# A runtime branch moved to the middle of the expert loop, with a deeper weight ring, in a two-layer decoder trunk

## The chip, the core and the metric

The kernel runs on one core of one Trainium2 chip, and its time is the device time in microseconds (us). Three executions took 850.05, 853.14 and 852.98 us; their median is 852.98 us. Engines are named as in the profile: PE (TensorE), PEld (its weight loads), DVE (VectorE), ACT (ScalarE), POOL (GpSimd) and SP (SyncE, which here does nothing but issue DMA transfers).

## The reference

One sequence of 256 tokens, 1024 features, passes two layers, all in float32. Layer 0 mixes tokens with a state-space scan, layer 1 with attention. Each layer ends in a mixture of 32 experts, of which every token uses two:

```python
for e in range(N_EXPERTS):                       # 32
    y = (jax.nn.silu(t @ w1[e]) * (t @ w3[e])) @ w2[e]
    out = out + gates[:, e:e + 1] * y            # gates: zero but for two experts per token
```

w1 and w3 are 1024x256 and w2 is 256x1024 for each expert, so the expert weights of a layer are 96 MB. Scale, shift and gate of each sub-layer come from `silu(c) @ ada_w`, with c one vector for the whole sequence.

## The kernel before

**The weight ring.** All large weights are cut into blocks of 1 MB, `[128, 2048]` in SBUF. A block is fetched by `fetch` (L66) into the next buffer of a ring (`new_slot`, L60): 10 buffers throughout (`ring=10`), to which a few more are added by `grow` while a stage has room (4 and then 5 more in the mixture of layer 0, 3 and then 4 more in that of layer 1). SP issues all these transfers in one queue; a transfer waits until its buffer's last reader is done, and for the landing of an earlier one that used the same of eight completion semaphores.

**The stages.** Layer 0 begins with the state-space part (the loop over 8 blocks below L990, most of its work on DVE), then an output gate, then its mixture; layer 1 has attention, then its mixture. At the very start SP is given the 8 blocks `ada00s`, then as many `win` blocks as the ring has room for (`ring - KD`), then the two tables `braw` and `craw` of the scan (L791, L792, 1 MB each), then the rest.

**The mixture** (`moe`). Every expert has a capacity of 32 tokens. Experts are taken in fours: `experts` loops over q = 0 to 7. In stage q `first` (L509) multiplies the gathered rows `xg` with 8 blocks `wa`, `second` (L524) with 4 blocks `wb`, DVE scales the result into `y` (L527) and `scatter` (L531) adds it into four PSUM banks `acc` with the one-hot matrix `Sc`. Meanwhile `place` (L459, L461) builds the one-hots of the next stage, `gather` (L473) multiplies the rows out for it, and `spread` multiplies its one-hots by the gates (L489, DVE), turns them on PE (L490) and copies them to `Sc`.

**The branch.** If an expert has more than 32 tokens, `overflow` (L538) computes the rest in the body of a runtime `If`, which is not entered with these inputs. It stands in program order in the last stage, q = 7, ahead of `first`: every engine reads the count (L622), compares and jumps. The body has its own transfers (SP, into the buffers of the tag "y") and its own matmuls, rows and copies; on the path that is not taken each engine instead raises its semaphores by what the body would have counted, after it has waited for what it had issued before.

**Order.** The scheduler of the framework orders each engine's instructions ahead of time by program order and by a model of their times; work may move past other work and past the branch, and the tiles of one tag are given out from a fixed number of buffers.

The line that the start depends on, and the buffers that the branch's body takes:

```python
for k in range(ring - KD if ring > KD else 0):
    prefetch("win", k)
...
w = mb[0].tile([128, 2, 512], F32, tag="y", name="ow", bufs=2)   # in overflow
```

## Time and profile before

| | us |
|---|---|
| median of three executions | 852.98 |
| the profiled execution | 851.51 |
| its span, first to last instruction | 849.7 |
| PE busy | 716.1 (84%) |
| DVE busy | 407.7 (48%) |
| DMA: 299.33 MB moved in the span | mean 352 GB/s |

The profiled execution is 1.47 us under the median, and 1.81 us longer than its span. PE is busy in most stages, but its busy time is an average over stages with different limits: what ends the waits differs between the state-space part, attention and the two mixtures. The DMA rate by slices of 21 us is the quickest way to tell them apart.

### The profile page before, as it was taken

The numbers are of one execution on the slowest core, as the hardware profiler recorded it, in microseconds if no ns is written. First come the engines' busy times: TensorE is split into PE (matmuls) and PEld (weight loads), VectorE is DVE, ScalarE is ACT, GpSimd is POOL, SyncE is SP. The second block draws the span as 40 slices with busy tenths as digits, with TensorE's granted clock in tenths as the row PEclk, the third lists the DMA queues.
The fourth block names the chain that finished last, engine by engine and source line by source line (L and its number), as shares of the span: only waits on it lengthen the run. The fifth ranks groups of instructions, "written<-read, shape, count | busy, mean of one in ns | idle before, by whom it ended". The sixth has DMA issues, their size and how long they took to land. (4 is left out here: it accounts for less than half of the span.)

```text
span 849.7 us, 13421 instructions
## 1 busy us (share of the span) xinstructions
PE 716.1 (84%) x5382; PEld 399.2 (47%) x5382; DVE 407.7 (48%) x1070; ACT 217.9 (26%) x498; POOL 51.5 (6%) x52
## 2 busy tenths in 40 slices
PE   3899999888999967866489999799888999887765
PEld 0676765663445312311245667788654443331211
DVE  7789999754223212110256579976644222221102
ACT  4334241442101101000143455566422111100100
POOL 2000000000000000000001104800200000000000
PEclk9999999999999998987699999999979999998888
DMA  9999676759999999999868988433889999999995
GB/s 372 426 424 390 248 297 250 306 214 424 427 427 426 425 427 427 426 425 426 341 252 324 341 299 297 154 145 115 316 330 370 426 427 425 427 427 427 426 425 213
DMA packets 41831, 299.33 MB, mean 352 GB/s; under 512 B 4632, under 2 KB 4760, under 8 KB 5664
## 3 DMA queue, kind: packets, MB, share of 16 engines
q1 hardware_dynamic: 41328, 297.13, 85.9%
q10 hardware_dynamic: 432, 1.25, 0.4%
q8 instruction: 46, 0.75, 0.3%
q14 instruction: 25, 0.20, 0.1%
HBM read 297.31 MB, written 1.05 MB: 351 GB/s over the span
## 5 line engine op out<-in xcount | busy, mean ns | idle before, releaser
L509 PE MATMUL mm<-w,xg 128*32 128x512 f32 x1024 | 138.0, 625 | 34.5 <-DMA w<-wa 23.0
L524 PE MATMUL mm<-w,aT 128*32 128x512 f32 x512 | 74.9, 705 | 16.2 <-DVE aT L499 7.4
L509 PEld LDWEIGHTS mm<-w,xg 128*32 128x32 f32 x1024 | 30.2, 111 | 116.8 <-issue 64.4
L531 PE MATMUL acc<-y,Sc 128*128 128x512 f32 x128 | 65.4, 636 | 22.6 <-DVE y L527 22.6
L1196 PE MATMUL acc<-ws,hn 128*128 128x512 f32 x288 | 76.4, 408 | 1.0 <-ACT hn L1164 0.8
L1126 DVE TENSOR_TENSOR ws<-w,ws 128x512 fp32r<-128x512 f32 x80 | 60.6, 764 | 30.2 <-ACT ws L1125 29.5
L473 PEld LDWEIGHTS mm<-Pr,h 128*128 128x128 f32 x512 | 61.4, 196 | 22.6 <-issue 20.6
L481 ACT ACTIVATE xg<-mm,sh,g 128x128 f32<-128x128 f32 x64 | 29.3, 457 | 162.8 <-PE mm L473 140.7
L515 DVE TENSOR_TENSOR a<-a,mm 128x256 f32<-128x256 f32 x16 | 6.7, 421 | 132.2 <-ACT a L514 132.2
L473 PE MATMUL mm<-Pr,h 128*128 128x128 f32 x512 | 65.9, 284 | 3.0 <-DVE Pr L461 3.0
L527 DVE TENSOR_TENSOR y<-mm,gbc 128x512 f32<-128x512 f32 x32 | 22.1, 692 | 92.8 <-PE mm L524 70.5
L1125 ACT ACTIVATE ws<-w 128x512 fp32r<-128x512 f32 x80 | 49.8, 628 | 63.3 <-PE acc L1196 42.4
L1196 PEld LDWEIGHTS acc<-ws,hn 128*128 128x128 f32 x288 | 51.6, 188 | 22.2 <-issue 5.5
L479 DVE TENSOR_SCALAR xg<-mm,g,sh 128x128 f32<-128x128 f32 x64 | 26.1, 407 | 73.7 <-ACT xg L481 73.7
L514 ACT ACTIVATE a<-mm 128x256 f32<-128x256 f32 x16 | 6.1, 383 | 192.8 <-PE mm L509 192.8
L531 PEld LDWEIGHTS acc<-y,Sc 128*128 128x128 f32 x128 | 22.6, 196 | 65.9 <-DVE y L527 38.3
L524 PEld LDWEIGHTS mm<-w,aT 128*32 128x32 f32 x512 | 15.4, 121 | 62.9 <-issue 35.3
L805 PE MATMUL mm<-hnT,w 128*64 128x128 f32 x512 | 32.2, 284 | 2.7 <-ACT hnT L278 2.7
L1390 PE MATMUL acc<-hn,ws 128*128 128x256 f32 x192 | 28.6, 307 | 6.6 <-DVE ws L1126 6.6
L805 PEld LDWEIGHTS mm<-hnT,w 128*64 128x64 f32 x512 | 30.4, 139 | 4.4 <-ACT hnT L278 3.7
L1390 PEld LDWEIGHTS acc<-hn,ws 128*128 128x128 f32 x192 | 26.3, 209 | 7.8 <-DVE ws L1126 7.5
L981 PE MATMUL acc<-w,uT 128*128 128x512 f32 x64 | 29.0, 596 | 0.7 <-ACT uT L970 0.7
(338 smaller groups left out, 963.5 us busy)
## 6 DMA issues: line engine op xcount, KB each, us to landing
w<-wa SPq DMA_DIRECT2D x128, 1024.0 KB, 19.6
w<-wb SPq DMA_DIRECT2D x64, 1024.0 KB, 19.6
w<-ada SPq DMA_DIRECT2D x36, 1024.0 KB, 10.8
w<-ada00s SPq DMA_DIRECT2D x8, 1024.0 KB, 13.6
w<-kvada SPq DMA_DIRECT2D x8, 1024.0 KB, 4.8
w<-win SPq DMA_DIRECT2D x4, 1024.0 KB
w<-ada00g SPq DMA_DIRECT2D x4, 1024.0 KB
w<-woutv SPq DMA_DIRECT2D x4, 1024.0 KB, 6.3
```

The lines of the kernel that those rows point to most:

```text
L473: PE.matmul(px[:, 128 * c4:128 * c4 + 128], h[:, i, 128 * c:128 * c + 128], Pr[:, i].rearrange("p a b -> p (a b)"), start=i == 0, stop=i == 1)
L479: V.tensor_scalar(xg[:, c], src, g[:, c:c + 1], sh[:, c:c + 1], op0=OP.mult, op1=OP.add)
L481: S.activation(xg[:, c], src, AF.Identity, bias=sh[:, c:c + 1], scale=g[:, c:c + 1])
L509: PE.matmul(ph[32 * s:32 * s + 32, :], xg[:, k, 32 * s:32 * s + 32], w[:, 512 * s:512 * s + 512], start=k == 0, stop=k == KD - 1)
L524: PE.matmul(py[32 * s:32 * s + 32, :], aT[:, 128 * f + 32 * s:128 * f + 32 * s + 32], w[:, 512 * s:512 * s + 512], start=f == 0, stop=f == 1)
L531: PE.matmul(acc[i][n], scs[q][:, 128 * i:128 * i + 128], y[:, 512 * n:512 * n + 512], start=q == 0, stop=q == NQ - 1, skip_group_check=True)
L805: PE.matmul(ps[64 * v:64 * v + 64, 128 * hh:128 * hh + 128], w[:, k, c0:c0 + 64], hnT[:, k, v::2], start=k == 0 and hh == 0, stop=k == KD ...
L981: PE.matmul(val[t][n], uT[:, m, 128 * t:128 * t + 128], wval[m // 2][:, c0:c0 + 512], start=m == 0, stop=m == 7)
L1125: S.activation(o[:, 0], w, AF.Copy)
L1126: V.tensor_tensor(o[:, 1], w, o[:, 0].bitcast(F32), op=OP.subtract)
L1196: PE.matmul(pk[i], src[:, k, a, 128 * i:128 * i + 128], w[:, b], start=k + a + b == 0, stop=k == KD - 1 and b == 1)
L1390: PE.matmul(po[:, 256 * m2:256 * m2 + 256], w[:, bb, kk, 128 * m2:128 * m2 + 128], hq[:, k, a, :], start=k + a + bb + m2 == 0, stop=k == K ...
```

## The change

The branch moves from q = 7 to q = 4, the middle of the loop. Its body's transfers no longer go into the tag "y" but into buffers of the weight ring (24 for one turn of its loop, where the mixtures have 21 and 19 of them); its normalised rows take the tag "y" instead of "xg", written by DVE; and it adds into `acc` instead of into `h`. "xg" has 2 buffers (was 3) and "P" 1 (was 2); `spread(q)` now stands ahead of `place(q + 1)`. The scratch for dynamic transfers is set to 1024 bytes, the vector `sc` is no longer copied 32 wide but read as a broadcast by PE, and the ring has 12 buffers instead of 10.

```diff
-def trunk(..., ring=10, ring2=4, ring3=5, ring4=3, ring5=4, lpb=2, TK=2):
+def trunk(..., ring=12, ring2=4, ring3=5, ring4=3, ring5=4, lpb=2, TK=2):
...
-    sc32 = const.tile([128, KD, 32], F32, name="sc32")
-    V.tensor_copy(sc32, sc[:, :, None].to_broadcast([128, KD, 32]))
+    def sc32(k):
+        return sc[:, k:k + 1].to_broadcast([128, 32])
...
-                PE.matmul(ps[32 * q:32 * q + 32, :], sc32[:, k, :], w[:, q], start=k == 0, stop=k == KD - 1)
+                PE.matmul(ps[32 * q:32 * q + 32, :], sc32(k), w[:, q], start=k == 0, stop=k == KD - 1)
...
-            return ma.tile([128, KD, 128], F32, tag="xg", name=n, bufs=3)
+            return ma.tile([128, KD, 128], F32, tag="xg", name=n, bufs=2)
...
-            P = mb[0].tile([128, 2, 4, CAP], F32, tag="P", name="P", bufs=2)
+            P = mb[0].tile([128, 2, 4, CAP], F32, tag="P", name="P", bufs=1)
...
-                hnT = [rows_tile("hnT") for _ in range(2)]
+                hnT = [mb[0].tile([128, KD, 128], F32, tag="y", name="hnT", bufs=2) for _ in range(2)]
                 for i in range(2):
-                    x = mb[0].tile([128, D], F32, tag="y", name="xn", bufs=2)
-                    V.tensor_scalar(x, h[:, i], rstd[:, i:i + 1], None, op0=OP.mult)
+                    x = mb[0].tile([128, 256], F32, tag="aT", name="dr", bufs=2)[:, 0:128]
+                    V.tensor_scalar(x, ident, rstd[:, i:i + 1], None, op0=OP.mult)
...
-                            PE.transpose(o, x[:, 128 * k:128 * k + 128], ident)
+                            PE.matmul(o, h[:, i, 128 * k:128 * k + 128], x, start=True, stop=True)
...
                         def part(name, j):
-                            w = mb[0].tile([128, 2, 512], F32, tag="y", name="ow", bufs=2)
+                            w = new_slot()[:, 0:1024].rearrange("p (k n) -> p k n", k=2)
                             nc.sync.dma_start(w, A[name][l, bass.ds(q, 1), 2 * j:2 * j + 2, :, c]
...
-                                add_gated(py[i], gbc, i, n, mb[0], "y", 2)
+                                for c2 in range(2):
+                                    r = slice(256 * c2, 256 * c2 + 256)
+                                    t = mb[0].tile([128, 256], F32, tag="aT", name="ot", bufs=2)
+                                    V.tensor_tensor(t, py[i][:, r], gbc[:, 512 * n + 256 * c2:512 * n + 256 * c2 + 256],
+                                                    op=OP.mult)
+                                    PE.matmul(acc[i][n][:, r], ident, t, start=False, stop=False,
+                                              skip_group_check=True)
...
-                if last:
+                if q == NQ // 2:
                     scatter(q - 1, y, 1)
                     overflow(nc.values_load(mosti[0:1, 0:1], min_val=0, max_val=T))
                 elif q:
...
+                spread(q)
                 if not last:
                     place(q + 1)
                     gather(q + 1)
-                spread(q)
                 aT = turned(a)
...
-    nc = bacc.Bacc("TRN2", target_bir_lowering=False, num_devices=1)
+    nc = bacc.Bacc("TRN2", target_bir_lowering=False, num_devices=1, dynamic_dma_scratch_size=1024)
```

## Rows read from the trace of the kernel before

**Rows 1.** The page: span, and GB/s in 40 equal slices.
```profile
span 849.7 us, 13421 instructions
...
GB/s 372 426 424 390 248 297 250 306 214 424 427 427 426 425 427 427 426 425 426 341 252 324 341 299 297 154 145 115 316 330 370 426 427 425 427 427 427 426 425 213
```

**Rows 2.** Two stretches: PE, PEld, DVE, ACT, POOL busy; clock, DMA share, GB/s.
```profile
50.00:150.00 100.00, 98.06 (x1384) 68.16 (x1380) 95.80 (x207) 33.61 (x93) 0.00 (x0) 1.00 0.77 310
285.50:401.90 116.40, 85.83 (x518) 27.79 (x516) 16.87 (x43) 7.02 (x16) 0.22 (x2) 0.88 1.01 426
```

**Rows 3.** Timeline of SP: first issue's start, time to the last one's end, count.
```profile
265.89 17.48 SPq L66 DMA_DIRECT2D w<-wa  x8
...
375.12 7.49 SPq L66 DMA_DIRECT2D w<-wb  x4
...
702.90 17.52 SPq L66 DMA_DIRECT2D w<-wa  x8
```

**Rows 4.** The page's DMA issues: count, KB each, median us to landing.
```profile
w<-wa SPq DMA_DIRECT2D x128, 1024.0 KB, 19.6
...
w<-kvada SPq DMA_DIRECT2D x8, 1024.0 KB, 4.8
```

**Rows 5.** The branch, line L538: ns min/median/max, first and last start in us.
```profile
L538 SPq EVENT_SEMAPHORE  x16: 17/17/17, 411.6 to 839.0; - x16
...
L538 PEldq COMPARE_BRANCH  x2: 545/3168/5790, 374.8 to 811.2; - x2
...
L538 SPq COMPARE_BRANCH  x2: 50/52/53, 392.4 to 818.5; - x2
```

**Rows 6.** Timeline, end of layer 0's mixture: start, length, [idle before <-releaser].
```profile
396.14 3.17 PE L524 MATMUL mm<-w,aT 128*32 128x512 f32 x16 [0.52 <-DVE aT L499]
...
412.35 0.69 DVE L527 TENSOR_TENSOR y<-mm,gbc 128x512 f32<-128x512 f32 x1 [16.27 <-SPq L538]
...
420.71 1.98 PE L531 MATMUL acc<-y,Sc 128*128 128x512 f32 x4 [0.82 <-DVE y L527]
```

**Rows 7.** Timeline, end of layer 1's mixture.
```profile
833.30 3.04 PE L524 MATMUL mm<-w,aT 128*32 128x512 f32 x16 [0.52 <-DVE aT L499]
...
839.21 0.69 DVE L527 TENSOR_TENSOR y<-mm,gbc 128x512 f32<-128x512 f32 x1 [5.97 <-SPq L538]
...
841.87 1.06 PE L524 MATMUL mm<-w,aT 128*32 128x512 f32 x8
...
843.75 1.98 PE L531 MATMUL acc<-y,Sc 128*128 128x512 f32 x4 [0.81 <-DVE y L527]
```

**Rows 8.** Lines L489 and L490 in layer 0's mixture, 190 to 420 us.
```profile
L489 DVE TENSOR_TENSOR P<-P,gates x16: 281/284/291, 204.5 to 326.3; 128x128 f32<-128x128 f32 x16
...
L490 PE MATMUL mm<-ident,P x16: 272/273/476, 215.4 to 384.1; 128*128 128x128 f32 x16
```

**Rows 9.** Timeline, the second y of stage 3 in layer 0 and layer 1.
```profile
287.05 0.69 DVE L527 TENSOR_TENSOR y<-mm,gbc 128x512 f32<-128x512 f32 x1 [3.10 <-PE mm L524]
...
724.57 0.69 DVE L527 TENSOR_TENSOR y<-mm,gbc 128x512 f32<-128x512 f32 x1 [3.10 <-PE mm L524]
```

**Rows 10.** Timeline of PE just behind the branch, layer 0 and layer 1.
```profile
380.92 2.95 PE L509 MATMUL mm<-w,xg 128*32 128x512 f32 x10 [3.60 <-issue]
...
817.43 3.64 PE L509 MATMUL mm<-w,xg 128*32 128x512 f32 x16 [4.75 <-PEq L538]
```

**Rows 11.** Timeline of the start: the scan's first table, and the loop's first product.
```profile
14.15 0.43 SPq L791 DMA_DIRECT2D braw<-s5b  x1
...
34.11 0.42 DVE L840 TENSOR_TENSOR abt<-braw,are 128x256 f32<-128x256 f32 x1 [1.59 <-DMA braw<-s5b]
...
48.23 0.69 DVE L918 TENSOR_TENSOR m<-mm,cosT 128x512 f32<-128x512 f32 x1 [2.22 <-PE mm L913]
```

**Rows 12.** Weight loads of a broadcast column (L206) and of a plain tile (L473).
```profile
L206 PEld LDWEIGHTS mm<-ident,sc x16: 190/190/192, 422.1 to 424.1; 128*128 128x128 f32 x16
...
L473 PEld LDWEIGHTS mm<-Pr,h 128*128 128x128 f32 x512 | 61.4, 196 | 22.6 <-issue 20.6
```

## The prediction

> **What bounds the kernel now.** I began with the page's DMA rate by slices. It stands at 424 to 427 GB/s for the first 60 us, through most of layer 0's mixture (slices 10 to 19) and of layer 1's (slices 32 to 39), and at 100 to 350 between them [rows 1]. Then two stretches by engine: in 100 us of the state-space loop DVE is busy 95.8 us, so DVE sets its pace; in the second half of layer 0's mixture DMA runs at 426 GB/s while PE is busy 85.8 of 116.4 us, so there the weights set it [rows 2]. The timeline of SP says the same: a load lands 19.6 us after its issue, which is eight 1 MB transfers in line [rows 4]. Stage 4's first block of layer 0 was issued at 265.89 and so landed at 285.5; the last of stage 7 at 375.12 + 7.49 - 0.33 = 382.3, landing at 401.9 [rows 3]. These are 47 blocks in 116.4 us, 2.48 each. Up to stage 3 it is PE's turn: the second y of stage 3 ends its wait by PE's product, at 287.05, when stage 4's first block had already landed [rows 3, 9].

> The branch shows last. In layer 0 PE's product for y was ready at 396.14 + 3.17 = 399.3, but DVE began at 412.35, ended by SP's line L538 [rows 6]. SP had reached the branch at 392.4 and raised its semaphores at 411.6 [rows 5]: 19.2 us, the time its eight transfers in line take to land. The branch's body writes buffers of tag "y" by DMA, so the y behind the branch waits for what SP raises. In layer 1 the same wait ends at 839.21, where the product was ready at 836.3 [rows 7].

> **The change, part by part.**

> 1. *The y wait goes.* Behind the branch y's buffers are no longer written by DMA. Without the wait, layer 0's end would run: y at 399.4 to 400.1, scatter (1.98) to 402.1, the products of the two last blocks (1.1 each; the last has landed at 401.9) to 404.3, y and scatter to 407.0. It ended at 420.71 + 1.98 = 422.7 [rows 6]: 15.7 us saved. In layer 1 the last scatter would begin at 841.3 in place of 843.75: y at 836.4, two products and a scatter by 840.6, y to 841.3; the last block has landed by 839.0, where SP's last semaphore is raised [rows 5, 7]. About 2.5 saved. Together -18.2. Late next are the weights themselves.

> 2. *The loads of stage 4 wait at the branch.* This decides. The body takes 24 ring buffers, more than there are, so each ring buffer's next load stands behind a reader in the body, and that reader's count is raised when PE passes the branch. Can loads be moved ahead of it? The trace shows one case of each kind: the multiplication by the gates for stage 7, which needs no new buffer, ran at 326.3, long before the branch; PE's transpose of its result, which needs a new PSUM buffer of the tag that the body also takes, ran at 384.1, behind it [rows 8]. Yet its input had been ready for 47 us, and PE idles in that stretch [rows 2]. I take the ring to be handled like that: stage 4's loads are issued only when PE is through. PE is through after stage 3's second y and its scatter: 287.05 + 0.69 + 0.06 + 1.98 = 289.8 in layer 0, 727.3 in layer 1 [rows 7, 9]. A load into an idle queue lands after 4.8 us, the median of `kvada` [rows 4]. So stage 4's first block lands at 289.8 + 0.1 + 4.8 = 294.7 instead of 285.5, and at 732.2 instead of 702.90 + 19.6 = 722.5 [rows 3]. From there the line of 48 blocks is unbroken and PE has a quarter of its time free [rows 2], so the ends move by the same: +9.2 and +9.7, +18.9 together. The bounds: -5 a layer if loads run ahead (first rival), +14 if PE's jump is slow too (second).

> 3. *Two more ring buffers.* They let SP be two blocks, 2 x 2.46 = 4.9 us, further ahead. But before the branch the last of stage 3 has then landed even earlier and DMA stands idle until PE arrives; and stages 0 to 3 do not wait for weights. In attention, DMA is far under its rate [rows 1]. I put 0, with -4.9 per mixture as the lower bound.

> 4. *The start.* Four `win` blocks instead of two stand ahead of the scan's tables in SP's queue, so these land 4.9 us later. DVE was already waiting for the first, 1.59 us until 34.11, and then had 2.22 us of idle time ahead of its first product at 48.23 [rows 11]. That gap and some shorter ones absorb about 2.7; I put +2.2, between 0 and 4.9. The loop behind it keeps DVE 96% busy and makes up nothing [rows 2].

> 5. *PE's own jump.* The branch instruction took 0.545 us in one layer and 5.79 in the other [rows 5], and PE's first product behind it waited 4.75 us for PE's sequencer in layer 1; in layer 0 a gap of 3.60 without a releaser came a few products later [rows 10]. Here the jump is issued before the last scatter ends and with DMA idle. I put +0.5 per layer; 0 to 4.4 each. [...]

> 6. *The small edits, 0 together.* A weight load of a broadcast column takes 190 ns, one of a plain tile 196 [rows 12], so reading `sc` as a broadcast costs PE nothing; it hides beside the products either way. One "P" and two "xg" buffers make `place(q + 1)` follow `spread(q)` in its own stage: DVE has 116.4 - 16.9 us idle there [rows 2] to cover it, and without that cover it would cost the four DVE operations, about 1 us a stage. The scratch size touches nothing in time: SP and ACT issue all transfers of this kernel, POOL none.

> The sum: -18.2 + 18.9 + 2.2 + 1.0 = +3.9 against the profiled execution's 851.51 (its span of 849.7 and 1.81 around it): **855.4 us**. That execution is 1.5 under the median of 852.98, so the forecast is 0.3% over the median. About 0.5%, 4.3 us, is what a measurement of this kernel can tell from no change.

> **The rivals.**

> *Loads run ahead of the branch, as they do now* (faster). For it: SP's loads of stage 7 and later were issued before its own branch at 392.4 in this trace, from 375.12 on [rows 3, 5]. Against it: those took buffers that the body did not. Then only SP's wait for its own eight transfers remains, and the queue restarts in 4.8 instead of 2.46, +2.4 a layer; the two buffers give -4.9 a layer. 851.5 - 18.2 + 2 x (2.4 - 4.9) + 2.2 gives **831 us**. A part of it, with some loads let through, lies between.

> *PE's jump stalls in both layers* (slower). The mechanism sits at the new place of the branch: SP's loads wait for PE, so what PE's sequencer loses there is lost by DMA too, while at the old place it was covered, since the weights were late anyway. Price: 4.75 against 0.4 us, +4.35 a layer in place of 0.5: 855.4 + 7.7 = **863 us**. It decides from the point where the jump takes more than the 1.5 us by which it is issued ahead of the scatter's end (811.2 against 817.43 - 4.75 = 812.7 in layer 1) [rows 5, 10]. For it, layer 1's 5.79; against it, layer 0's 0.545 and the idle queue.

> *The start costs its whole 4.9 us* (slower): 855.4 + 2.7 = **858 us**. For it: DVE 96% busy; against it: the 2.22 gap.

> **How the numbers follow.** My forecast 0.45, loads running ahead 0.27, slow jumps 0.20, the whole start 0.08. The forecast's own range is 849 to 859, of which I put 0.36 within 0.5% of the median, 0.07 above and 0.02 below. Faster: 0.27 + 0.02 = 0.29. Slower: 0.07 + 0.20 + 0.08 = 0.35. Same: 0.36. The range runs from 836, inside the first rival's upper part (0.12 of its 0.27), to 864: 0.45 + 0.12 + 0.16 (of the second rival's 0.20) + 0.08 = 0.81.

> **What would show it.** Right: DVE's y after the branch waits for PE alone; DMA idle for some 12 to 15 us ahead of stage 4 in each mixture; SP's first load of stage 4 released by PE; the scan's first table landing near 39 us; layer 0's mixture ending near 419 in place of 422.7, layer 1's about 7 later against its own beginning. Wrong: an unbroken DMA rate across the middle of the mixtures (first rival), or a branch instruction of PE over 4 us in both layers (second). The forecast also fails if stages 0 to 3 become shorter, since the branch is then reached earlier.

## The result and the profile after

The changed kernel takes 879.35 us (median of 4 runs, 877.41 to 880.9) against 852.91 for the kernel before in the same comparison: a ratio of 1.0305 (95% interval 1.0273 to 1.0338). It is slower by 3%, where 855.4 had been forecast with a range of 836 to 864. Line numbers of the changed kernel are one higher around the mixture and seven higher in the state-space part: the branch is L539, the y L528, the scatter L532.

First the page of the changed kernel: its span, and the DMA rate in 40 slices of 21.9 us.

```profile
span 877.2 us, 13392 instructions
...
GB/s 374 424 428 306 320 190 260 308 250 356 426 427 426 92 362 427 426 426 427 427 426 426 308 302 261 192 152 108 344 335 423 426 426 91 373 429 426 427 427 266
```

Where [rows 1] had an unbroken 424 to 427 through both mixtures, slices 14 and 34 now stand at 92 and 91. At a full rate of 427 these two and their neighbours (362 and 373) miss 20.5 us of DMA in layer 0 and 20.0 in layer 1. That is the hold which step 2 of the prediction described, and it is longer than the 12 to 15 us expected.

How much of the time this explains shows once the span is cut at two events of each layer: the write of `mosti` by DVE, from which the routing is known, and the end of the last scatter by PE. The timeline of DVE, kernel before:

```profile
196.30 0.15 DVE L438 CAST mosti<-most 128x1 int32<-128x1 f32 x1
...
632.22 0.15 DVE L438 CAST mosti<-most 128x1 int32<-128x1 f32 x1
```

The timeline of DVE, changed kernel:

```profile
210.13 0.15 DVE L439 CAST mosti<-most 128x1 int32<-128x1 f32 x1
...
648.23 0.15 DVE L439 CAST mosti<-most 128x1 int32<-128x1 f32 x1
```

The timeline of PE, changed kernel; the last scatters of the kernel before end at 422.69 and 845.73 [rows 6, 7]:

```profile
433.13 1.98 PE L532 MATMUL acc<-y,Sc 128*128 128x512 f32 x4 [1.21 <-DVE y L528]
...
871.21 1.98 PE L532 MATMUL acc<-y,Sc 128*128 128x512 f32 x4 [0.81 <-DVE y L528]
```

The differences of these times, in us, with the forecast's terms beside them:

| part | before | after | change | forecast |
|---|---|---|---|---|
| start, to `mosti` of layer 0 | 196.3 | 210.1 | +13.8 | +2.2 |
| mixture of layer 0 | 226.4 | 225.0 | -1.4 | -6.0 |
| attention and routing of layer 1 | 209.5 | 213.1 | +3.6 | 0 |
| mixture of layer 1 | 213.5 | 225.0 | +11.5 | +7.7 |
| output | 4.0 | 4.0 | 0 | 0 |
| span | 849.7 | 877.2 | +27.5 | +3.9 |

The mixtures miss the forecast by 8.4 us together, attention by 3.6, and the start by 11.6. So the largest error arises in the start, most of it in the first 100 us, far ahead of the branch that the prediction was mostly about.

The branch's own rows, line L539 (ns min/median/max, first and last start in us):

```profile
L539 SPq EVENT_SEMAPHORE  x16: 17/17/17, 281.5 to 731.8; - x16
L539 SPq COMPARE_BRANCH  x2: 50/52/53, 272.1 to 712.8; - x2
...
L539 PEldq COMPARE_BRANCH  x2: 3502/3696/3890, 304.8 to 742.5; - x2
...
L539 PEldq EVENT_SEMAPHORE  x2: 51/51/51, 308.4 to 746.5; - x2
```

In layer 0 SP reaches the branch at 272.1 and raises its eight semaphores from 281.5 to 291.5, yet it issues nothing until PE is through. This is the timeline of SP around the branch of layer 0:

```profile
264.36 7.71 SPq L66 DMA_DIRECT2D w<-wb  x4
308.47 5.42 SPq L66 DMA_DIRECT2D w<-wa  x8
```

PE's semaphore goes up at 308.4, and the first load of stage 4 is issued at 308.47. The timeline of PE shows what follows, with the last scatter ahead of the branch and the first product behind it, in layer 0 and in layer 1:

```profile
303.91 1.98 PE L532 MATMUL acc<-y,Sc 128*128 128x512 f32 x4 [0.81 <-DVE y L528]
313.81 1.93 PE L510 MATMUL mm<-w,xg 128*32 128x512 f32 x8 [7.92 <-DMA w<-wa]
...
742.01 1.98 PE L532 MATMUL acc<-y,Sc 128*128 128x512 f32 x4 [0.81 <-DVE y L528]
751.70 1.94 PE L510 MATMUL mm<-w,xg 128*32 128x512 f32 x8 [7.70 <-DMA w<-wa]
```

PE stands for 7.9 and 7.7 us: its own jump of 3.5 and 3.9, and a load into an empty queue. The scatters end at 305.9 and 744.0 and PE's semaphore goes up at 308.4 and 746.5, so the jump adds 2.5 us to the hold in each layer. PE also comes to the branch later than before, as the second y of stage 3 in the timeline of DVE shows for both layers:

```profile
303.17 0.69 DVE L528 TENSOR_TENSOR y<-mm,gbc 128x512 f32<-128x512 f32 x1 [3.96 <-PE mm L525]
...
741.27 0.69 DVE L528 TENSOR_TENSOR y<-mm,gbc 128x512 f32<-128x512 f32 x1 [3.96 <-PE mm L525]
```

That is 93.0 us after the routing in both; before it was 90.7 and 92.4 [rows 9].

The y wait of 16.27 us [rows 6] is gone; at the end of layer 0 DVE waits for PE's product alone, as its timeline shows:

```profile
427.34 0.69 DVE L528 TENSOR_TENSOR y<-mm,gbc 128x512 f32<-128x512 f32 x1 [3.71 <-PE mm L525]
```

Now the start. The timeline of DVE has the first table, the scan loop's first product, and the sum of a gate's product with its bias (L192):

```profile
39.61 0.43 DVE L847 TENSOR_TENSOR abt<-braw,are 128x256 f32<-128x256 f32 x1 [7.35 <-DMA braw<-s5b]
...
53.56 0.69 DVE L925 TENSOR_TENSOR m<-mm,cosT 128x512 f32<-128x512 f32 x1 [0.86 <-PE mm L920]
...
74.68 0.68 DVE L192 TENSOR_TENSOR rows<-mm,rows 128x512 f32<-128x512 f32 x1
```

The table comes 5.5 us later than in [rows 11], the first product 5.3. The engine that connects the two is ACT. Its timeline in the kernel before, which the prediction didn't read:

```profile
40.48 2.62 ACTq L184 DMA_DIRECT2D rows<-gbias  x2
43.15 0.51 ACT L852 ACTIVATE ab<-braw 128x128 f32<-128x128 f32 x2 [11.20 <-DMA w<-ada00g]
```

and in the changed kernel:

```profile
45.40 2.62 ACTq L185 DMA_DIRECT2D rows<-gbias  x2
48.07 0.39 ACT L814 ACTIVATE uT<-mm 128x256 f32<-128x256 f32 x1 [16.39 <-DMA w<-ada00g]
```

ACT has two small transfers of `gbias` to issue. Its idle time around them, 11.20 and 16.39 us, is ended by the landing of a 1 MB block `ada00g`, and the second issue begins 2.4 us behind the first in both kernels (42.87 and 47.79), where a block takes 2.46 at 426 GB/s. ACT's copies for PE, and through PE all of the loop, stand behind that. Another 5 us go at 75 us, where PE waits for the sum of L192 (it ends at 75.36; the view names ACT). The timeline of PE has both stops:

```profile
48.70 1.11 PE L868 MATMUL mm<-ident,ab 128*128 128x128 f32 x4 [5.63 <-ACT ab L859]
...
75.47 3.55 PE L198 MATMUL mm<-rows,pick 128*128 128x512 f32 x4 [3.34 <-ACT rt L936]
```

A part of the start's loss goes with TensorE's granted clock. Here are three stretches of the changed kernel, then one of the kernel before (length; busy time of PE, PEld, DVE, ACT, POOL; granted clock, DMA share, GB/s):

```profile
48.00:54.80 6.80, 5.91 (x42) 5.21 (x43) 3.93 (x12) 2.99 (x9) 0.00 (x0) 0.50 1.01 428
75.30:78.70 3.40, 3.23 (x4) 1.18 (x4) 3.36 (x10) 1.86 (x3) 0.00 (x0) 0.50 0.13 53
164.00:167.40 3.40, 3.40 (x66) 2.97 (x56) 0.27 (x1) 0.18 (x1) 0.00 (x0) 0.50 0.56 169
...
33.60:187.00 153.40, 146.90 (x1844) 108.77 (x1841) 131.56 (x280) 55.88 (x142) 0.00 (x0) 1.00 0.77 310
```

The granted clock stands at 0.50 from the end of both stops, in which PE was idle for 5.6 and 3.3 us, and once more at 164 us; in the kernel before it is 1.00 from 33.6 to 187 us. The timeline of PE has the same 64 products at either level, changed kernel first:

```profile
163.74 3.42 PE L975 MATMUL mm<-m,cz 128*32 128x128 f32 x64
...
151.82 1.95 PE L968 MATMUL mm<-m,cz 128*32 128x128 f32 x64
```

These products alone account for 1.5 of the 13.8 us; what the other two stretches cost was not separated from the stops.

### The profile page after: what moved, and what is told of

Same layout as the page of the kernel before. It is cut to its first block, busy times and chain, and to the rows that moved or that the text cites. A ratio compares the mean times of both kernels' runs of the same rounds, so it can differ in the third digit from the quotient of the medians.

```text
span 877.2 us, 13392 instructions
## 1 busy us (share of the span) xinstructions
PE 735.0 (84%) x5382; PEld 400.0 (46%) x5382; DVE 410.5 (47%) x1069; ACT 218.6 (25%) x498; POOL 57.8 (7%) x52
## 5 line engine op out<-in xcount | busy, mean ns | idle before, releaser
L510 PE MATMUL mm<-w,xg 128*32 128x512 f32 x1024 | 146.0, 651 | 49.3 <-DMA w<-wa 49.2
L510 PEld LDWEIGHTS mm<-w,xg 128*32 128x32 f32 x1024 | 27.8, 112 | 139.5 <-DMA w<-wa 69.8
L474 PE MATMUL mm<-Pr,h 128*128 128x128 f32 x512 | 65.4, 282 | 11.4 <-DVE Pr L462 11.4
L532 PE MATMUL acc<-y,Sc 128*128 128x512 f32 x128 | 63.8, 622 | 8.5 <-DVE y L528 8.5
L1203 PEld LDWEIGHTS acc<-ws,hn 128*128 128x128 f32 x288 | 51.1, 188 | 23.9 <-issue 7.1
L528 DVE TENSOR_TENSOR y<-mm,gbc 128x512 f32<-128x512 f32 x32 | 22.1, 692 | 73.2 <-PE mm L525 72.9
L493 DVE COPY Sc<-mm 128x256 f32<-128x256 f32 x16 | 6.8, 425 | 93.3 <-PE mm L491 93.3
L532 PEld LDWEIGHTS acc<-y,Sc 128*128 128x128 f32 x128 | 22.2, 193 | 51.6 <-issue 29.0
L1130 POOL TENSOR_TENSOR w<-w,gbc 128x512 f32<-128x512 f32 x16 | 32.5, 2066 | 0.0
## 6 DMA issues: line engine op xcount, KB each, us to landing
w<-ada00s SPq DMA_DIRECT2D x8, 1024.0 KB, 16.4
```

The costliest lines, as they stand in the source:

```text
L474: PE.matmul(px[:, 128 * c4:128 * c4 + 128], h[:, i, 128 * c:128 * c + 128], Pr[:, i].rearrange("p a b -> p (a b)"), start=i == 0, stop=i == 1)
L510: PE.matmul(ph[32 * s:32 * s + 32, :], xg[:, k, 32 * s:32 * s + 32], w[:, 512 * s:512 * s + 512], start=k == 0, stop=k == KD - 1)
L532: PE.matmul(acc[i][n], scs[q][:, 128 * i:128 * i + 128], y[:, 512 * n:512 * n + 512], start=q == 0, stop=q == NQ - 1, skip_group_check=True)
L1130: G.tensor_tensor(w, w, gate, op=OP.mult)
L1203: PE.matmul(pk[i], src[:, k, a, 128 * i:128 * i + 128], w[:, b], start=k + a + b == 0, stop=k == KD - 1 and b == 1)
```

## The experiments

All ratios are to the kernel before, run beside. The parts of each span are cut as above, from the profiled execution:

| kernel | time | ratio, 95% interval | start | mixture 0 | attention | mixture 1 |
|---|---|---|---|---|---|---|
| before | 852.9 | | 196.3 | 226.4 | 209.5 | 213.5 |
| after | 879.35 | 1.0273 to 1.0338 | 210.1 | 225.0 | 213.1 | 225.0 |
| e1_two_win | 873.88 | 1.0191 to 1.0271 | 208.7 | 224.0 | 212.4 | 223.7 |
| e2_no_branch | 831.38 | 0.9704 to 0.9764 | 209.2 | 207.1 | 206.4 | 204.1 |
| e3_own_tag | 840.58 | 0.9808 to 0.9885 | 208.5 | 207.8 | 208.4 | 210.0 |
| e4_before_no_branch | 832.26 | 0.9687 to 0.9792 | 198.4 | 209.4 | 207.7 | 210.9 |
| e5_ring10 | 856.03 | 1.0022 to 1.0067 | 196.8 | 222.1 | 209.0 | 222.9 |
| e6_own_tag_gbias_early | 828.94 | 0.9700 to 0.9755 | 197.8 | 210.7 | 206.2 | 209.6 |
| e7_own_tag_ring10 | 838.00 | 0.9818 to 0.9892 | 196.6 | 212.1 | 206.1 | 212.6 |
| e8_last_stage | 854.36 | 0.9991 to 1.0050 | 210.3 | 218.0 | 209.2 | 213.2 |
| e9_no_branch_ring10 | 829.87 | 0.9682 to 0.9785 | 196.6 | 211.0 | 205.9 | 209.3 |
| e10_pool_queue | 822.38 | 0.9604 to 0.9677 | 196.7 | 204.4 | 209.0 | 204.7 |
| e11_gbias_early | 864.97 | 1.0095 to 1.0171 | 196.3 | 227.2 | 213.4 | 224.2 |
| e12_before_pool_queue | 837.91 | 0.9763 to 0.9872 | 196.5 | 210.9 | 212.2 | 211.3 |

### The start: e1, e5 and e11

**e1_two_win.** Four `win` blocks ahead of the tables become two again, and the ring stays at 12.

```diff
-    for k in range(ring - KD if ring > KD else 0):
+    for k in range(2):
         prefetch("win", k)
```

> The changed kernel with one edit: only two blocks of `win` are fetched ahead of the scan's tables, as the kernel before did, with the ring still at 12. Theory S (the start is lost to the order of SP's loads: two more 1 MB blocks stand ahead of the tables, 4.9 us, and the state-space part gives up more behind that): the routing is known near 197.3 us as before instead of 211.1, and the time falls by 12 to 14 us, to 865 to 867. Rival T (the start is lost to the other edits of that part, above all the multiplications that read `sc` as a broadcast column): within 3 us of 879.35.

It gave 5.5 us, and the routing was known at 208.7: neither theory. The first table is loaded as early as in the kernel before, and yet ACT stands as long as in the changed one. Its timeline in e1_two_win:

```profile
45.45 2.60 ACTq L185 DMA_DIRECT2D rows<-gbias  x2
48.10 0.51 ACT L859 ACTIVATE ab<-braw 128x128 f32<-128x128 f32 x2 [16.29 <-DMA w<-ada00g]
```

So the late table isn't the cause; theory S had the wrong place.

**e5_ring10.** The changed kernel with `ring=10`, nothing else.

> The changed kernel with 10 ring buffers in place of 12, all else as changed, the branch in the middle too. Theory S2 (what the start loses comes from the longer ring: SP runs two loads further ahead of ACT, and ACT, which issues two small transfers of `gbias`, is held until later loads have landed, 45.4 instead of 40.5): the first product of the scan is back near 48.3 us, the routing is known at 197 to 199, and the time falls by 12 to 14 us to 865 to 868. Rival T (the broadcast column in the multiplications): the routing stays at 209 to 211, and the time within 3 us of 879.35. Both: the holes in the middle of the mixtures stay, shorter by up to 4.9 us on their early side, with no gain from that.

It took 856.03 us, 23.3 less than with 12 buffers and more than the 12 to 14 of theory S2; the start went back to 196.8, so rival T falls, and the broadcast column costs nothing that can be seen. ACT's timeline here is that of the kernel before to 0.1 us:

```profile
40.57 2.60 ACTq L185 DMA_DIRECT2D rows<-gbias  x2
43.22 0.51 ACT L859 ACTIVATE ab<-braw 128x128 f32<-128x128 f32 x2 [11.02 <-DMA w<-ada00g]
```

and DVE's timeline has the first product at its old time and the sum of L192 13.6 us earlier than in the changed kernel, ahead of a scan instead of behind it:

```profile
48.30 0.69 DVE L925 TENSOR_TENSOR m<-mm,cosT 128x512 f32<-128x512 f32 x1 [2.22 <-PE mm L920]
...
61.06 0.68 DVE L192 TENSOR_TENSOR rows<-mm,rows 128x512 f32<-128x512 f32 x1
```

Counted in the timelines of SP and ACT, 23 transfers are issued ahead of the first `gbias` in the kernel before and in e5_ring10, 25 in the changed kernel and in e1_two_win. In all four the transfer eight places ahead of that `gbias` is an `ada00g` block, which is what ACT stands for: the first of them in the kernel before, in e5_ring10 and, two places later in line, in the changed kernel, the third in e1_two_win. With 12 buffers two more loads fit ahead of `gbias`, whichever they are, and ACT stands two loads, 4.9 us, longer. This fits four kernels; that an issue waits for the eighth transfer before it was not tried by itself.

**e11_gbias_early.** The changed kernel with the two `gbias` transfers issued at the very start into a tile of their own; the gate's function takes that tile.

```diff
+    rows00 = sp.tile([128, 512], F32, name="rows00")
+    G.memset(rows00, 0.0)
+    for n in range(2):
+        nc.scalar.dma_start(rows00[32 * n:32 * n + 1, :], A["gbias"][0, n:n + 1, :])
     for k in range(KD):
         prefetch("ada00s", k)
...
-    side = [ada_gate_pe("ada00g", 0, 0, gb00, True),
+    side = [ada_gate_pe("ada00g", 0, 0, gb00, True, rows00),
```

> The changed kernel with one edit: the two small transfers of `gbias` are issued at the very start into a tile of their own. Body of the branch on the ring, 12 ring buffers, branch in the middle. Theory L (with the longer ring the start is lost to ACT, which stands at that issue, and to nothing else): the routing known near 198 us in place of 210.1, the time 879.35 less 11 to 13: 866 to 869, mixtures and attention as in the changed kernel (225, 213, 225). Rival V (the 9 us that the longer ring costs behind the start, by e5_ring10, also come from the shifted order of the start): 855 to 861.

The routing was known at 196.3 and the time fell by 14.4 us to 864.97, with four `win` blocks still ahead of the tables. That is theory L, a little more than it asked. Mixtures and attention stay as long as in the changed kernel, against rival V. The second stop at 75 us went too; it came of the same shift of order. PE's four products behind the sum of L192 took 1.99 us here and 1.98 in e5_ring10, as in the kernel before (1.98), where the changed kernel took 3.55 at a granted clock of 0.50. What stays open is why the longer ring costs another 9 us behind the start, 864.97 against 856.03: in the profiled executions 5.1 in layer 0's mixture, 4.4 in attention, 1.3 in layer 1's. Of the 5.1 and the 1.3, 2.0 and 1.2 have been lost by the second y of stage 3, before the branch.

### The hold at the branch: e2, e9, e3 and e8

**e2_no_branch.** The call of `overflow` is left out.

```diff
-                    overflow(nc.values_load(mosti[0:1, 0:1], min_val=0, max_val=T))
```

> The changed kernel without the branch: the part for overfull experts is left out altogether, and nothing stands in the middle of the mixtures. Theory H (SP's loads are held at the branch until PE has passed it, and PE's jump adds to that): no hole in the DMA rate within a mixture. Layer 0's mixture takes the 225.4 us of before less the y wait of 15.7, less 0 to 4.9 for the two ring buffers, layer 1's 216.8 less 2.5 less the same, against 225 and 228 in the changed kernel: 30 to 39 us less, 840 to 849. Rival O (the mixtures are longer because of the order `spread` then `place` and the fewer buffers): a gain of less than 11 us, above 868.

831.38 us, 48.0 less than the changed kernel; the mixtures shrank by 17.9 and 20.9, attention by 6.7. That is theory H, though the gain is some 9 us more than its 840 to 849 asked.

**e9_no_branch_ring10.** The same with `ring=10`.

> The changed kernel without the branch and with 10 ring buffers: the part for overfull experts is left out altogether. Theory H (the branch in the middle, with 10 buffers too, costs the hold of the loads and PE's jump, and the other edits cost nothing): mixtures of about 209 and 211 us as in e4_before_no_branch, 222.1 and 222.9 in e5_ring10, so 856.0 less 25, plus or minus 3: 828 to 834. Rival O (the order `spread` then `place`, one `P` and two `xg` buffers make the mixtures longer): 836 or more.

829.87, inside theory H's 828 to 834. Against e4_before_no_branch, 832.26, the small edits (order of `spread` and `place`, fewer `P` and `xg`, broadcast column) cost nothing that can be told where no branch stands. Against e2_no_branch the start is 12.6 shorter and the mixtures are 3.9 and 5.2 longer: without the branch the longer ring gives back most of what it takes from the start (831.38 against 829.87).

**e3_own_tag.** The branch's body loads into a buffer of its own.

```diff
-                            w = new_slot()[:, 0:1024].rearrange("p (k n) -> p k n", k=2)
+                            w = mb[0].tile([128, 2, 512], F32, tag="ow", name="ow", bufs=1)
```

> The changed kernel with one edit: the body of the branch loads its weights into one buffer of a tag of its own (4 KB) and takes no ring buffer. The branch stays in the middle. Theory H1 (the loads are held because they use ring buffers that the body also takes): SP then waits at the branch only for its own transfers in line, the hole in the DMA rate shrinks from 20 to 22 us to about 5 in both layers, and the time falls by about 2 x 16 us, to 843 to 853. Rival H2 (SP is held until PE is through the branch whatever the body writes): within 3 us of 879.35. A value between would say that PE's jump, 3.5 and 3.9 us, is what is left.

840.58, 38.8 less with the branch still in the middle: theory H1, and 2.4 us below its range. The page's DMA rate:

```profile
GB/s 371 426 425 304 345 165 252 282 344 282 426 427 426 426 424 426 350 425 429 426 426 427 424 302 270 152 188 125 293 313 410 427 426 428 419 367 378 425 428 272
```

The holes of 92 and 91 are gone; 350 in slice 17 and 367 and 378 in slices 36 and 37 are left, some 4 to 6 us of DMA per layer, where SP waits for its own transfers in line. PE's jump has become longer in the same kernel (line L539):

```profile
L539 PEldq COMPARE_BRANCH  x2: 5942/6760/7579, 303.2 to 719.1; - x2
```

It costs nothing in layer 0, where the mixture is as short as without a branch (207.8 and 207.1), since the weights are what is waited for; in layer 1 the mixture stays 5.9 longer than without a branch (210.0 and 204.1), and how much of that is the jump was not separated. So the hold comes from the shared buffers, and not from the place of the branch alone.

**e8_last_stage.** The changed kernel with the branch put back.

```diff
-                if q == NQ // 2:
+                if last:
```

> The changed kernel with the branch put back to the last stage, all else as changed (its body on the ring, 12 ring buffers). Theory D (a hold at the branch costs the distance by which the loads run ahead of PE there: 15 to 20 us in the middle, where PE sets the pace of stages 0 to 3, and little at the last stage, where PE waits for each load): 831.4, the time without a branch, plus 5 to 9 us per layer, so 841 to 850. Rival W (at the last stage the loads are held by SP's own eight transfers in line, 16 to 19 us, as the y was): 862 to 870. If the place makes no difference: within 3 us of 879.35.

854.36, between the two: 25.0 less than in the middle, but dearer than theory D. The rows of L539 show the same hold at the new place:

```profile
L539 SPq EVENT_SEMAPHORE  x16: 17/17/17, 380.0 to 807.5; - x16
L539 SPq COMPARE_BRANCH  x2: 50/52/53, 360.9 to 787.9; - x2
...
L539 PEldq COMPARE_BRANCH  x2: 3315/3356/3396, 383.4 to 810.7; - x2
```

In layer 0 SP's last semaphore goes up at 380.5, PE's at 386.9. The mixtures are 10.9 and 9.1 us longer than in e2_no_branch, in the middle 17.9 and 20.9. Counted from the routing, the first load behind the branch is issued 34.3 and 34.1 us later than in e2_no_branch when the branch stands in the middle, and 23.9 and 24.1 later when it stands in the last stage: the loads run further ahead of PE in the middle, and the hold costs more there.

### The old wait: e4 and e12

**e4_before_no_branch.** The kernel before without its call of `overflow`.

> The kernel before without the branch: the part for overfull experts is left out. It prices the y wait that the prediction put at 15.7 and 2.5 us. Theory Y (the wait is on the path in full): 852.9 less 18.2 is 834.7, so 832 to 838. Rival Z (the weights of attention land during the wait, so that part of it is given back later): 840 to 853, with the attention part longer than its 210.2 us of before by what is given back.

832.26: theory Y. The mixtures shrank by 17.0 and 2.6 us, where the prediction had put the y wait at 15.7 and 2.5.

**e12_before_pool_queue.** The kernel before with the transfers in the branch's body on another queue.

```diff
-                            nc.sync.dma_start(w, A[name][l, bass.ds(q, 1), 2 * j:2 * j + 2, :, c]
+                            nc.gpsimd.dma_start(w, A[name][l, bass.ds(q, 1), 2 * j:2 * j + 2, :, c]
```

> The kernel before with one edit: the transfers in the body of its branch (last stage, buffers of tag y) are issued by POOL's queue in place of SP's. Theory Y (the y behind the branch waits for nothing but SP's raise, which comes after its own transfers in line have landed; POOL has none and passes the branch as soon as the routing is known): the y wait goes in both layers, mixtures near 209 and 211 us as in e4_before_no_branch, the time 832 to 836. Rival K (the y waits at the branch for another engine too, PE's jump or DVE's place in order): 840 to 853.

837.91: a little over theory Y's 832 to 836, and short of rival K's 840. Its mechanism shows plainly in the timeline of DVE, at the y that had begun at 412.35 [rows 6]:

```profile
399.59 0.69 DVE L527 TENSOR_TENSOR y<-mm,gbc 128x512 f32<-128x512 f32 x1 [3.75 <-PE mm L524]
```

Prediction and run agree on when this y can begin, 399.4 and 399.59. The mixtures are as expected; attention took 212.2 us in place of some 208.

### Towards a faster kernel: e6, e7 and e10

**e6_own_tag_gbias_early** joins e3_own_tag and e11_gbias_early.

> The kernel of e3_own_tag (ring 12, the body's weights in one buffer of their own) with one more edit: the two small transfers of `gbias` are issued at the very start into a tile of their own, so ACT has nothing to issue in the scan's part. Theory L (ACT stands at that issue, 16.4 us, and its copies for PE stand behind it): the first product falls from 53.0 us to 48 to 50, and the time from 840.6 to 828 to 836, by how much of the second stop (near 72 to 84 us) goes too. Rival M (the tables themselves, 4.9 us later, set the start whatever ACT does): first product at 52.5 or later, time within 3 us of 840.6.

828.94, theory L: first product at 48.52, routing at 197.8.

**e7_own_tag_ring10** is e3_own_tag with `ring=10`.

> The kernel of e3_own_tag with 10 ring buffers in place of 12. Theory S2 (the start is lost to the longer ring, and the mixtures need no longer ring once the branch holds no loads): routing known at 197 to 199, mixtures as in e3_own_tag, so 840.6 less 11 to 13: 827 to 830. Rival U (with 10 ring buffers the branch's wait for SP's own transfers empties the line for longer, up to 4.9 us per mixture): 830 to 838.

838.00, though its four runs spread from 833.2 to 842.3: the edge of rival U. The start came back (196.6), but the mixtures of its profiled execution are 4.3 and 2.6 us longer than in e3_own_tag. Where the branch doesn't hold the loads, the two more buffers are worth something.

**e10_pool_queue** is e6_own_tag_gbias_early with the body's transfers on POOL's queue, as in e12.

> The kernel of e6_own_tag_gbias_early with one more edit: the transfers in the body of the branch are issued by POOL's queue, which has nothing else to do there, in place of SP's, so that SP has no part in the branch. Theory Q (what is left of the branch's price is SP's wait for its own transfers in line, about 5 us of idle DMA per layer): no dip of the DMA rate in the middle, mixtures near 207 and 204 us as in e2_no_branch, the time 819 to 824. Rival J (what is left is PE's jump, 6 to 7.6 us, which no queue changes): 826 to 830.

822.38, theory Q. The branch's rows (now L540) show that POOL comes to it 1.0 us after the routing of layer 0 (196.7) and takes 0.045 us, and that PE's jump is still slow, 5.8 and 6.0 us:

```profile
L540 POOLq COMPARE_BRANCH  x2: 45/45/45, 197.7 to 610.8; - x2
...
L540 PEldq COMPARE_BRANCH  x2: 5832/5917/6002, 291.6 to 704.5; - x2
```

The page's DMA rate has no dip in either mixture:

```profile
GB/s 370 426 427 423 387 221 246 289 274 357 425 427 427 427 424 426 425 428 426 428 425 427 390 291 267 158 170 130 287 311 417 427 427 425 424 426 426 427 426 254
```

and the timeline of PE behind the branch of layer 0 has PE waiting for its own sequencer, and no longer for a load:

```profile
298.00 3.45 PE L511 MATMUL mm<-w,xg 128*32 128x512 f32 x16 [5.50 <-PEq L540]
```

Mixtures of 204.4 and 204.7 us are those without a branch (207.1 and 204.1). This kernel beats the one before by 3.6% (0.9604 to 0.9677): it is the change with three of its side effects taken away.

## Why the prediction was wrong

**The step that failed is the fourth, the start.** It read: "That gap and some shorter ones absorb about 2.7; I put +2.2, between 0 and 4.9." The start took 13.8 us more, 2.8 times the upper bound. The step counted only the delay of the tables, and looked for what would take it up in DVE's idle time. e11 shows that the delay of the tables is indeed taken up: with four `win` blocks ahead of them the routing is known at 196.3. The loop that "makes up nothing" made it up: in e11 the table is 5.5 us late, and from 101 us on the loop's products are back at their old times. What isn't taken up is ACT's stand at its issue of `gbias`. The longer ring makes it some 5 us longer, and the order that comes of it moves one sum (L192) behind a scan, which costs another 5; 1.5 more go with the granted clock of 0.50 at 164 us. ACT's stand showed in the trace of before: 11.20 us of its idle time ended by a load that ACT doesn't read. The step took DVE's 96% as the loop's limit, but PE was busy 98.06 of the same 100 us [rows 2], and it is PE that stood, for 5.6 and 3.3 us, and then ran at a granted clock of 0.50. The third step, "Two more ring buffers ... I put 0", was blind in the same way: it asked only what longer lead SP gains, not which other engine shares its line. Between e5 and the changed kernel those two buffers cost 23.3 us; without the branch they are worth 3.9 and 5.2 in the mixtures (e2 against e9), about the lower bound of -4.9 that the step gave.

**The hold (step 2) was right in mechanism and short in size.** "Stage 4's loads are issued only when PE is through" is what the SP timeline shows, to 0.1 us, and e3 shows that the shared buffers are the reason. The first rival, loads that run ahead, is out for this kernel, and becomes true as soon as the body has its own buffer. Idle DMA was 20.5 and 20.0 us, against 12 to 15. In e5, with 10 buffers, slices 14 and 34 (21.4 us each, 156 and 177 GB/s) give 13.6 and 12.5: the forecast's figure holds for the ring of before, in part by luck, since e5's includes a jump of 3.6 us, and the longer ring empties the line earlier: SP comes to the branch 62.0 us after the routing in the changed kernel, 67.0 in e5.

In size the step fell short by three terms. In layer 0 it had stage 4's first block land at 294.7, 98.4 us after the routing; PE's first product began on it at 313.81, 103.7 after. Of these 5.3 us, 2.3 come from stages 0 to 3, 2.5 from the jump and 0.5 from the load, which took 5.3 from its issue to that product in place of 4.9. Counted from the routing the block is then 14.5 later than before, where 9.2 had been forecast, and 14.5 less the 15.7 of the y wait is close to the measured -1.4. One reading in the step is off, without effect on the sum: by [rows 8] the input of PE's transpose had been ready for 57.5 us, not 47.

**PE's jump (step 5) was under-priced.** "I put +0.5 per layer; 0 to 4.4 each": the jump took 3.5 and 3.9 us in the changed kernel, just short of the 4 us that the prediction named as the second rival's sign, and 2.5 of it in each layer lie behind the scatter's end, where loads and PE both wait for it. So the second rival's mechanism came true in both layers, at a little over half of its price of 4.35. The step also counted on the idle DMA for a short jump, which was its author's assumption: no row of the kernel before shows it, with 0.545 us in one layer and 5.79 in the other, while DMA ran at 437 and 421 GB/s. In the runs the jump was shorter where the loads were held, 3.3 to 3.9 us against 5.8 to 7.6 where they stayed in line, and yet not short. The sum for the mixtures was +1.7; e5 has +5.1 (-4.3 and +9.4), the changed kernel +10.1.

**The y wait (step 1) was right**: 15.7 and 2.5 forecast, 17.0 and 2.6 in e4, 15.5 and 2.2 in e12.

**The small edits (step 6) were right at 0**, by e9 against e4. PE now waits 11.4 us in all for `Pr`, where it was 3.0, and 11.0 of these lie in stages 0 to 3, where PE sets the pace; the cover that the step named, DVE's idle time, was read in stages 4 to 7. Still, with 10 buffers (e5) the second y of stage 3 comes 91.0 and 91.8 us after the routing, against 90.7 and 92.4 before, so these waits cost next to nothing there; the 93.0 of the changed kernel come with the longer ring.

**Not foreseen and not settled**: attention took 205.9 to 213.4 us over these kernels, though no edit but the ring's length and the broadcast column reaches it; it was 3.6 longer in the changed kernel.

So the mixtures alone, as forecast, come to a slowdown that can hardly be told from none, and e5 measures one (1.0022 to 1.0067). Most of the 3%, 23.3 of 26.4 us, is the longer ring beside this branch, which the prediction had priced at 0 and 2.2.

## What to carry to other kernels

In this kernel the ring buffers that a branch also uses, though it is never taken, held the loads behind it until PE had passed it: 20.5 and 20.0 us of DMA in the changed kernel, and 38.8 us of its time against e3_own_tag. The price was higher where the loads ran further ahead: 48.0 us in the middle and 23.0 in the last stage, against e2_no_branch. So give the body its own buffer, and a queue that has nothing else to do, which took another 6.6 us off (e6 to e10). What that costs when the branch is taken was not measured, since these inputs never take it. When a ring is made longer, look at every engine that issues a transfer among the ring's loads, however small: here ACT, with two transfers of 2 KB, stood 16.39 us for a load in place of 11.20, and the loop's first product behind it came 5.3 us later. An idle time that is ended by a transfer which the engine doesn't read is the row to look for.
